# Two stages of a mixture of experts at 376 columns instead of 384, with eight tokens served by fetched rows

## The chip, the cores and the metric

The kernel runs on one core of a Trainium2 chip. The metric is the device time of one execution in microseconds (us), taken as the median of three runs. A core has engines that run side by side, each with its own instruction stream in a fixed order: TensorE (PE, matrix products; PEld is its weight load), VectorE (DVE), ScalarE (ACT), GpSimd (POOL) and SyncE (SP, which here only issues transfers). DMA transfers run on 16 engines of their own.

## The reference, cut to what matters

The reference is two stacked transformer parts on 512 tokens of width 1024. The change lies in the feed-forward part of the first, `peer_ffn`: for every token, 8 heads each choose the best 16 of 16384 single-neuron experts, and the token's output is the sum over its 128 chosen experts.

```python
eidx = jnp.take_along_axis(cidx, fpos, axis=-1).reshape(C, PEER_HEADS * PEER_TOPK)   # 128 experts a token
g = jax.nn.softmax(fv, axis=-1).reshape(C, PEER_HEADS * PEER_TOPK)
u = u_tab[eidx]
a = jax.nn.gelu(jnp.einsum('ted,td->te', u, hb).astype(jnp.float32), approximate=False)
coef = (g * a).astype(hb.dtype)
vv = v_tab[eidx]
return jnp.einsum('te,ted->td', coef, vv)
```

## The kernel before

The kernel has four parts in order: `phase_a` (attention), `phase_peer` (the experts), `phase_conv` and `phase_nsa`. Every large product is done three times on halves of fp32 numbers (`mm3`, lines 178 to 180: high by high, low by high, high by low). Weights arrive as units of 128 x 1024 numbers by SP (`_load`), and each is split (`_split`): ACT writes the high half `whi` (line 102) and DVE the low half `wlo` (line 103).

`phase_peer` serves the first 384 tokens (`ND`) densely and the last 128 by fetching rows:

- **Dense, stage U.** 128 units of the table u; each is multiplied with all 384 tokens (8 blocks of 128 x 3 products of 384 columns), and ACT applies the gelu (line 1215). The results go to DRAM as `Ad`, in 32 groups of 4 units.
- **Gates.** For each token a 128 x 128 table of gate values is made as a product of two one-hot matrices (`gates`, `flush`, line 1105). DVE and ACT build the one-hots (lines 1119, 1123, 1124 and 1126), four tokens at a time. Twelve chunks of 32 tokens come out; ten go to DRAM as `Gd`, the last two stay in `near`.
- **Dense, stage V.** For each of the 128 units of v, `weight` multiplies gates (`gg`, loaded from `Gd`, 640 KB for a group of 4 units, plus two small products for the near chunks, line 1257) with the gelu values, splits the result (`w_hi`, `w_lo`), and 8 x 3 products of 384 columns add into all eight PSUM banks `y`. The v units arrive in a ring of eight 512 KB pieces in memory that stage U's activations held until its last product.
- **Fetched tokens.** `gather` issues 256 indirect transfers on POOL (line 1141): 128 rows of u, then of v, one row for each of the 128 tokens, 512 KB each. A DVE instruction consumes each (lines 1149 and 1159). Three buffers hold u rows, three hold v rows.

What runs beside the products is queued as generators. `pump` and `pump2` take steps from them by credits: `BU` of background work and `GU` (in stage V `GV`) of fetching for each unit; a fetch costs 1.2. A scheduler then orders every engine's instructions by its own simulated timeline, so the order on an engine can differ from the order of the code. `in_turn` adds an order constraint without a wait between engines: before, each fetch's consumer is kept behind the split that was emitted last.

## Time and profile before

| quantity | value |
|---|---|
| median of three runs | 2426.43 us (2426.17 to 2426.85) |
| the profiled execution, its own time | 2425.24 us |
| its span, first to last instruction | 2423.5 us |
| PE busy | 2381.2 us, 98% |
| DVE busy | 1870.4 us, 77% |
| ACT busy | 1149.8 us, 47% |
| mean granted clock of TensorE | 0.991 |

Shares are of the span, so an engine at 77% can be full in one stage and half empty in another. Stage U runs from about 419 to 1037 us and stage V from 1037 to about 1570 us. A busy PE is not a PE at its peak, since its instructions overlap; the spacing of their starts tells the pace. Rows below come from the profile's page and from questions put to the same trace; a line number such as L103 is that of the kernel's file.

### The profile page before, as it was taken

To read this page: it belongs to the slowest core of one execution; us is meant where nothing else is said; L and a number is where in the kernel's file an instruction comes from. 1 tells how busy PE (TensorE), PEld (TensorE's weight loads), DVE (VectorE), ACT (ScalarE), POOL (GpSimd) and SP (SyncE) were. 2 spreads that over 40 slices of the span, in tenths; PEclk is the share of its full clock that TensorE was granted. 3 is DMA by queue.
4 is the path that set the end of the run, shared out by engine and by line. 5 is a ranking of instruction groups with operands and counts; after the bars stand their busy time and mean duration, and the time that the engine had idled before them with its cause. 6 is when DMAs were issued, how large, how long until landed. Compare 5 with 4: busy or idle time off the path is not lost.

```text
span 2423.5 us, 37687 instructions
## 1 busy us (share of the span) xinstructions
PE 2381.2 (98%) x13637; PEld 2163.1 (89%) x13637; DVE 1870.4 (77%) x4198; ACT 1149.8 (47%) x2336; POOL 373.6 (15%) x366
## 2 busy tenths in 40 slices
PE   7999999999999999999999999999999999999998
PEld 5887888999999999999999999988888888887777
DVE  7898579999998978878888887865555436796774
ACT  4467433434777858733333333432222233555772
POOL 0011000014323343324332221100000001000000
PEclk8999999999999999999999999999999999999999
DMA  7460252469989998899999899432223225211002
GB/s 277 145 221 7 75 174 84 161 235 319 335 293 338 349 350 329 276 394 329 382 342 360 319 352 313 165 104 96 96 98 100 98 96 186 91 62 61 1 1 79
DMA packets 170937, 490.47 MB, mean 202 GB/s; under 512 B 15472, under 2 KB 62512, under 8 KB 169088
## 3 DMA queue, kind: packets, MB, share of 16 engines
q1 hardware_dynamic: 123744, 295.48, 35.1%
q0 software_dynamic: 44992, 189.68, 21.5%
q10 hardware_dynamic: 2016, 2.91, 0.4%
q8 instruction: 108, 1.77, 0.3%
q14 instruction: 77, 0.63, 0.1%
HBM read 437.15 MB, written 50.86 MB: 201 GB/s over the span
## 4 chain that ended last, share of the span: by engine, by line
PE 91%; DVE 4%; DMA 2%; ACT 1%; issue 1%; SPq 0%; DVEq 0%; ACTq 0%
PE mm L179 8%; PE mm L180 8%; PE mm L178 8%; PE s L180 8%; PE s L178 8%; PE s L179 8%; PE pt L178 4%; PE pt L180 4%; PE pt L179 4%; PE gp L1105 4%; PE z L178 2%; PE z L180 2%; PE z L179 2%; PE o L1756 2%; PE o L180 2%; PE o L178 2%
## 5 line engine op out<-in xcount | busy, mean ns | idle before, releaser
L102 ACT ACTIVATE whi<-wraw 128x1024 fp32r<-128x1024 f32 (+2 forms) x292 | 305.2, 1046 | 535.0 <-PE mm L179 170.5
L103 DVE TENSOR_TENSOR wlo<-wraw,whi 128x1024 fp32r<-128x1024 f32 (+2 forms) x292 | 351.8, 1206 | 100.4 <-ACT whi L102 98.2
L179 PE MATMUL mm<-act,whi 128*128 128x384 f32 (+2 forms) x1176 | 403.8, 344 | 4.0 <-DVE act L378 4.0
L180 PE MATMUL mm<-act,wlo 128*128 128x384 f32 (+2 forms) x1176 | 402.7, 343 | 0.1
L178 PE MATMUL mm<-act,whi 128*128 128x384 f32 (+2 forms) x1176 | 399.6, 343 | 0.7 <-DVE xres L868 0.7
L102 ACT ACTIVATE whi<-act 128x1024 fp32r<-128x1024 f32 x126 | 133.6, 1061 | 327.9 <-issue 314.0
L179 PEld LDWEIGHTS mm<-act,whi 128*128 128x128 f32 x1176 | 222.7, 189 | 8.1 <-DVE act L378 4.2
L180 PEld LDWEIGHTS mm<-act,wlo 128*128 128x128 f32 x1176 | 222.7, 189 | 4.4 <-DVE wlo L103 0.5
L178 PEld LDWEIGHTS mm<-act,whi 128*128 128x128 f32 x1176 | 220.6, 189 | 4.8 <-issue 0.8
L103 DVE TENSOR_TENSOR wlo<-act,whi 128x1024 fp32r<-128x1024 f32 x126 | 154.2, 1225 | 82.8 <-ACT whi L102 81.5
L1141 POOL DMA_INDIRECT ug<-in_peer_u_rows_dram,eiG x128 | 158.9, 1241 | 363.8 <-DVE ug L1149 246.4
L1141 POOL DMA_INDIRECT vg<-in_peer_v_rows_dram,eiG x128 | 158.3, 1237 | 295.3 <-DVE yG L1159 186.7
L179 PE MATMUL s<-w_lo,whi 128*128 128x384 f32 x512 | 171.1, 334 | 0.3 <-DVE w_lo L224 0.3
L178 PE MATMUL s<-w_hi,whi 128*128 128x384 f32 x512 | 170.4, 334 | 0.8 <-ACT ga L1215 0.6
L180 PE MATMUL s<-w_hi,wlo 128*128 128x384 f32 x512 | 170.5, 334 | 0.0
L1159 DVE SCALAR_TENSOR_TENSOR yG<-vg,gG,yG 128x1024 f32<-128x1024 f32 x127 | 162.7, 1281 | 7.1 <-DMA vg<-in_peer_v_rows_dram,eiG 6.9
L1149 DVE SCALAR_TENSOR_TENSOR ug<-ug,hG 128x1024 f32<-128x1024 f32 x128 | 155.8, 1220 | 6.6 <-DMA ug<-in_peer_u_rows_dram,eiG 6.5
L178 PE MATMUL s<-act,whi 128*128 128x512 f32 x344 | 134.3, 391 | 0.0
L180 PE MATMUL s<-act,wlo 128*128 128x512 f32 x344 | 134.0, 390 | 0.2 <-DVE wlo L103 0.2
L179 PE MATMUL s<-act,whi 128*128 128x512 f32 x344 | 133.6, 389 | 0.0
L1119 DVE TENSOR_SCALAR oh<-iof,idxT 128x128 f32<-128x128 f32 x384 | 117.8, 354 | 9.0 <-PE gp L1105 8.8
L1105 PE MATMUL gp<-oh,oh 128*128 128x128 f32 x768 | 115.0, 274 | 0.0
(700 smaller groups left out, 5722.0 us busy)
## 6 DMA issues: line engine op xcount, KB each, us to landing
wraw<-in_peer_u_dram SPq DMA_DIRECT2D x128, 512.0 KB, 5.0
act<-in_peer_v_rows_dram SPq DMA_DIRECT2D x126, 512.0 KB, 7.2
wraw<-in_a_in_dram SPq DMA_DIRECT2D x64, 512.0 KB, 3.2
Ad<-ga POOLq DMA_DIRECT2D x30, 768.0 KB, 7.4
ga<-Ad SPq DMA_DIRECT2D x30, 768.0 KB, 9.8
Gd<-gc POOLq DMA_DIRECT2D x10, 2048.0 KB, 8.9
gg<-Gd SPq DMA_DIRECT2D x32, 640.0 KB, 7.8
wraw<-in_ada_w_dram SPq DMA_DIRECT2D x32, 512.0 KB, 4.5
```

The lines of the kernel that those rows point to most:

```text
L102: self.first = first = self.nc.scalar.activation(hi[:, :n], r[:, :n], AF.Copy)
L103: self.last = self.nc.vector.tensor_tensor(lo[:, :n], r[:, :n], hi[:, :n].bitcast(F32), op=OP.subtract)
L178: mm(out, lh, rh, start=start, stop=False)
L179: mm(out, lh, rl, start=False, stop=False)
L180: self.product = mm(out, ll, rh, start=False, stop=stop)
L1105: nc.tensor.matmul(gp[:, j, :], o1, o2, start=True, stop=True)
L1119: nc.vector.tensor_scalar(o1, iof, idxT[:, 0, t:t + 1], idxT[:, 2, t:t + 1], op0=OP.is_equal, op1=OP.mult)
L1141: nc.gpsimd.indirect_dma_start(out=t, out_offset=None, in_=tab, in_offset=bass.IndirectOffsetOnAxis(ap=eiG[:, j:j + 1], axis=0))
L1149: c.in_turn(nc.vector.scalar_tensor_tensor(u, u, 1.0, hG, op0=OP.mult, op1=OP.mult, accum_out=aG[:, j:j + 1]))
L1159: op = nc.vector.scalar_tensor_tensor(yG, v, gG[:, j:j + 1], yG, op0=OP.mult, op1=OP.add)
L1756: nc.tensor.matmul(o[64 * h:64 * h + 64, t], V[:, b, v], pair[h][br][:, b * P:(b + 1) * P], start=False, stop=br == 1 and b == qb, skip_gr ...
```

## The change

- `ND` falls from 384 to 376: every product of stages U and V has 376 columns. The eight tokens 376 to 383 are served by rows: each token's 128 experts are spread over 16 groups of partitions (`RX` = 16), so that 8 fetches of u and 8 of v (`gather_x`) do all eight tokens. 32 small transfers on POOL place their indices and gates; `rows_of_x` makes 16 copies of their activations by 8 sums and 8 transposes; at the end 8 small products with `fold` sum the 16 groups into `y`.
- All fetches share four buffers (`NFE`), the credits are 1.75 in stage U and 1.3 in stage V, and the split that is emitted is kept behind the consumer of the fetch that was emitted six (stage V: four) places earlier (`lag`, `paced`, `in_step`).
- The one-hots of four tokens are made by two DVE comparisons of 128 x 512, and ACT scales four of them by the gate.
- The near gates (now two chunks of 28 tokens) are applied in one product instead of two.
- Gates arrive for two groups in one transfer of 1280 KB (two buffers instead of three), and v units in pairs of 1 MB.
- `w_out`'s first four products take their k blocks in the order 0, 1, 2, 4, 5, 6, 7, 3.

```diff
...
-ND = 384
+ND = 376
+N3 = S - P
+XT = N3 - ND
+RX = P // XT
...
-GU, BU, GUL, BUL, GV = 1.6, 2.4, 1.6, 2.4, 1.6
+GU, BU, GUL, BUL, GV = 1.75, 2.4, 1.75, 2.4, 1.3
...
-VB, GB, NGA, W1, FO = 8, 3, 2, 4, 8
+VB, GB, NGA, W1, FO = 8, 2, 2, 4, 8
+NFE = 4
...
         if self.vring is not None and key[0] == "V":
+            if i in self.raw:
+                return
             t = self.vring[self.vnext % len(self.vring)]
             self.vnext += 1
+            if key[1] % 2 == 0:
+                self.raw[i], self.raw[i + 1], view, n = t[:, :1024], t[:, 1024:], t, 2048
+            else:
+                self.raw[i], view = t[:, 1024:], t[:, 1024:]
         else:
-            t = self.wpool.tile([P, 1024], F32, name="wraw", bufs=self.LOAD_AHEAD + 2)
-        view = t[:, :n]
+            t = self.raw[i] = self.wpool.tile([P, 1024], F32, name="wraw", bufs=self.LOAD_AHEAD + 2)
+            view = t[:, :n]
+            if key[0] == "V" and key[1] % 2 == 0:
+                src = src[:, 0, :]
...
         self.last = self.nc.vector.tensor_tensor(lo[:, :n], r[:, :n], hi[:, :n].bitcast(F32), op=OP.subtract)
+        if self.lag is not None and len(self.paced) >= self.lag:
+            self.in_turn(self.last, self.paced[-self.lag])
...
+    def in_step(self, op):
+
+        self.in_turn(op)
+        self.paced.append(op)
...
-    def gemm_w(self, key, out, act, k0=0, start=True, stop=True, pump=3.0):
+    def gemm_w(self, key, out, act, k0=0, start=True, stop=True, pump=3.0, ks=range(KD)):
 
         hi, lo = self.get(key, pump)
-        for k in range(KD):
+        for k in ks:
             c = slice(k * P, (k + 1) * P)
             self.mm3(out, (hi[:, c], lo[:, c]), (act[0][:, k0 + k, :], act[1][:, k0 + k, :]),
-                     start and k == 0, stop and k == KD - 1)
+                     start and k == ks[0], stop and k == ks[-1])
...
-            c.gemm_w(("w_out", m), outs[m], mixed)
+            c.gemm_w(("w_out", m), outs[m], mixed, ks=(0, 1, 2, 4, 5, 6, 7, 3))
...
+            if (tb + 1) * P > ND:
+                eix = pool.tile([P, P], I32, name="eix", bufs=1)
+                nc.vector.tensor_copy(eix, ev)
+                for r in range(RX):
+                    to, sl = slice(r * XT, (r + 1) * XT), slice(r * P // RX, (r + 1) * P // RX)
+                    nc.gpsimd.dma_start(eiX[to, :], eix[P - XT:P, sl])
+                    nc.gpsimd.dma_start(gX[to, :], gv[P - XT:P, sl])
+                c.later2(gather_x())
...
+            tt = slice(tb * P, min(ND, (tb + 1) * P))
+            nc.scalar.activation(idxT[:, :, tt], pt[:, :3 * P].rearrange("p (i t) -> p i t", i=3)[:, :, :tt.stop - tt.start], AF.Copy)
...
-            for ch in range(4):
-                gc = gcpool.tile([P, P, 32], F32, name="gc", bufs=2)
-                near[tb * 4 + ch] = gc
+            for n in range(tb * 4, min(NC_, tb * 4 + 4)):
+                gc = gc2[:, n % 2]
                 prev = None
-                for q in range(8):
-                    hots = []
+                nq = (32 if n < NF_ else NL) // 4
+                for q in range(nq):
+                    t0 = min(n, NF_) * 32 + max(n - NF_, 0) * NL + q * 4
+                    os = [rpool.tile([P, 4, P], F32, name=n, bufs=2) for n in ("oh1", "oh2")]
+                    for i, o in enumerate(os):
+                        nc.vector.tensor_tensor(o, iof[:, None, :].to_broadcast([P, 4, P]),
+                                                idxT[:, i, t0:t0 + 4, None].to_broadcast([P, 4, P]), op=OP.is_equal)
                     for j in range(4):
-                        t = tb * P + ch * 32 + q * 4 + j
-                        o1 = rpool.tile([P, P], F32, name="oh1", bufs=6)
-                        o2 = rpool.tile([P, P], F32, name="oh2", bufs=6)
...
+                        nc.scalar.activation(os[1][:, j, :], os[1][:, j, :], AF.Copy, scale=idxT[:, 2, t0 + j:t0 + j + 1])
+                    hots = [(os[0][:, j, :], os[1][:, j, :]) for j in range(4)]
...
+                flush(prev, gc, nq - 1)
+                if n < NF_:
+                    nc.gpsimd.dma_start(Gd[n], gc.rearrange("p i t -> p (i t)"))
...
+        def rows(tab, idx, j):
+            t = gpool.tile([P, D], F32, name="fetched", bufs=NFE)
+            nc.gpsimd.indirect_dma_start(out=t, out_offset=None, in_=tab,
+                                         in_offset=bass.IndirectOffsetOnAxis(ap=idx[:, j:j + 1], axis=0))
+            return t
...
-                    u = rows(a["peer_u_rows"], j, "ug", 3)
-                    c.in_turn(nc.vector.scalar_tensor_tensor(u, u, 1.0, hG, op0=OP.mult, op1=OP.mult,
+                    u = rows(a["peer_u_rows"], eiG, j)
+                    c.in_step(nc.vector.scalar_tensor_tensor(u, u, 1.0, hG, op0=OP.mult, op1=OP.mult,
...
-                    c.in_turn(op)
+                    c.in_step(op)
...
+        def rows_of_x():
+
...
+                    hs = pool.tile([P, RX, XT], F32, name="stmp", bufs=2)
+                    hh, hl = [act[i][:, kk, None, ND:N3].bitcast(F32).to_broadcast([P, RX, XT]) for i in range(2)]
+                    nc.vector.tensor_tensor(hs, hh, hl, op=OP.add)
...
+                    nc.tensor.transpose(pt[:, k * P:(k + 1) * P], hs.rearrange("p r t -> p (r t)"), c.ident)
...
+        def gather_x():
+
+            n = P // RX
+            for j in range(n):
+                u = rows(a["peer_u_rows"], eiX, j)
+                c.in_step(nc.vector.scalar_tensor_tensor(u, u, 1.0, hX, op0=OP.mult, op1=OP.mult,
+                                                         accum_out=aX[:, j:j + 1]))
+                yield 1.2
...
+        c.later(rows_of_x())
...
+        c.lag = 6
...
-        c.vring = [t.rearrange("p k t -> p (k t)")[:, i * 1024:(i + 1) * 1024] for t in c.act.two(F32) for i in range(4)]
+        c.vring = [t.rearrange("p k t -> p (k t)")[:, i * 2048:(i + 1) * 2048] for t in c.act.two(F32) for i in range(2)]
...
-            gg = vpool.tile([P, NF_, 4, 32], F32, name="gg", bufs=GB)
-            nc.sync.dma_start(gg.rearrange("p c i t -> p c (i t)"),
-                              Gd[0:NF_, :, grp * P:(grp + 1) * P].rearrange("c p n -> p c n"))
+            if grp % 2 == 0:
+                two = vpool.tile([P, NF_, 8, 32], F32, name="gg", bufs=GB)
+                nc.sync.dma_start(two.rearrange("p c i t -> p c (i t)"),
+                                  Gd[0:NF_, :, grp * P:(grp + 2) * P].rearrange("c p n -> p c n"))
+                gates_of[grp], gates_of[grp + 1] = two[:, :, 0:4], two[:, :, 4:8]
...
-            for n in range(NF_, NC_):
-                t = slice(n * 32, n * 32 + 32)
-                nc.vector.tensor_tensor(w[:, t], near[n][:, order[g] * 4 + j, :], ga[:, j, t], op=OP.mult)
+            nc.vector.tensor_tensor(w[:, F_:].rearrange("p (c t) -> p c t", c=2), gc2[:, :, order[g] * 4 + j, 0:NL],
+                                    ga[:, j, F_:].rearrange("p (c t) -> p c t", c=2), op=OP.mult)
...
+        fold = vpool.tile([P, XT], F32, name="fold")
+        nc.vector.tensor_reduce(fold, c.ident.rearrange("p (r t) -> p t r", r=RX), axis=AX.X, op=OP.add)
         weight(0)
+        c.lag = 4
...
-                    nc.tensor.transpose(y[m][:, ND:S], yG[:, m * P:(m + 1) * P], c.ident)
+                    nc.tensor.matmul(y[m][:, ND:N3], yX[:, m * P:(m + 1) * P], fold, start=True, stop=True)
+                    nc.tensor.transpose(y[m][:, N3:S], yG[:, m * P:(m + 1) * P], c.ident)
...
-        c.add_unit(("V", i), v[:, 4 * GRP_V[i // 4] + i % 4, :], 1024)
+        e = 4 * GRP_V[i // 4] + i % 4
+        c.add_unit(("V", i), v[:, e:e + 2, :] if i % 2 == 0 else v[:, e, :], 1024)
...
```

## Rows read from the trace of the kernel before

**Rows 1.** Busy time by stage: PE, PEld, DVE, ACT, POOL, clock, DMA share, GB/s.

```profile
419.00:1037.00 618.00, 617.57 (x3839) 617.11 (x3837) 562.33 (x1377) 402.34 (x954) 187.46 (x176) 1.00 0.83 297
1037.00:1570.00 533.00, 532.32 (x3070) 531.62 (x3071) 443.60 (x830) 190.35 (x262) 152.43 (x120) 1.00 0.91 331
```

**Rows 2.** PE's instructions by shape: count, busy us, mean ns.

```profile
L179 PE MATMUL mm<-act,whi 128*128 128x384 f32 x1024 | 348.2, 340 | 0.0
...
L1105 PE MATMUL gp<-oh,oh 128*128 128x128 f32 x768 | 115.0, 274 | 0.0
```

**Rows 3.** PE in order of time: start us, us; 256, 512 and 384 columns, unbroken runs.

```profile
276.92 0.28 PE L180 MATMUL ps<-act_hi,wlo 128*128 128x256 f32 x1
...
279.40 0.28 PE L180 MATMUL ps<-act_hi,wlo 128*128 128x256 f32 x1
...
404.68 0.39 PE L179 MATMUL mm<-act,whi 128*128 128x512 f32 x1
...
407.40 0.40 PE L179 MATMUL mm<-act,whi 128*128 128x512 f32 x1
...
1020.21 0.34 PE L179 MATMUL mm<-act,whi 128*128 128x384 f32 x1
...
1022.81 0.34 PE L179 MATMUL mm<-act,whi 128*128 128x384 f32 x1
```

**Rows 4.** The chain that ended last: start us, us; eight gate instructions.

```profile
616.15 0.89 PE gp L1105 x8
```

**Rows 5.** Busy time in three parts of stage U, columns as in rows 1.

```profile
419.00:544.00 125.00, 125.00 (x728) 125.00 (x727) 124.93 (x458) 50.69 (x69) 12.68 (x13) 1.00 0.57 196
544.00:740.00 196.00, 196.00 (x1209) 195.90 (x1209) 190.09 (x398) 124.84 (x290) 68.06 (x64) 1.00 0.89 320
740.00:1037.00 297.00, 296.57 (x1906) 296.21 (x1904) 247.31 (x523) 226.82 (x595) 106.72 (x99) 1.00 0.89 326
```

**Rows 6.** DVE's groups in stage U: count, busy us, mean ns, idle before.

```profile
L103 DVE TENSOR_TENSOR wlo<-wraw,whi 128x1024 fp32r<-128x1024 f32 x127 | 155.1, 1221 | 30.1 <-ACT whi L102 29.8
L1119 DVE TENSOR_SCALAR oh<-iof,idxT 128x128 f32<-128x128 f32 x384 | 117.8, 354 | 9.0 <-PE gp L1105 8.8
L1149 DVE SCALAR_TENSOR_TENSOR ug<-ug,hG 128x1024 f32<-128x1024 f32 x67 | 81.5, 1221 | 6.6 <-DMA ug<-in_peer_u_rows_dram,eiG 6.5
L1159 DVE SCALAR_TENSOR_TENSOR yG<-vg,gG,yG 128x1024 f32<-128x1024 f32 x63 | 80.7, 1282 | 7.1 <-DMA vg<-in_peer_v_rows_dram,eiG 6.9
...
L1126 DVE TENSOR_SCALAR oh<-iof,idxT 128x128 f32<-128x128 f32 x96 | 29.1, 304 | 0.0
```

**Rows 7.** DVE's groups by shape, whole trace.

```profile
L592 DVE TENSOR_TENSOR raw<-raw,rsd 128x512 f32<-128x512 f32 x8 | 5.0, 686 | 0.0
```

**Rows 8.** Fetch consumers, lines 1149 and 1159, at the start of stage V (DVE busy).

```profile
1037.00:1200.00 163.00, 30.56 (x51) 1.00 1.00 372
...
1037.00:1200.00 163.00, 19.23 (x15) 1.00 1.00 372
```

**Rows 9.** POOL's group of plain transfers; a u fetch and its us to landing.

```profile
L1217 POOL DMA_DIRECT2D Ad<-ga x30 | 17.1, 569 | 241.3 <-ACT ga L1215 229.9 <-ACT ohd L1123 7.5 <-ACT oh L1124 3.9
...
ug<-in_peer_u_rows_dram,eiG POOLq DMA_INDIRECT x128, 7.2
```

**Rows 10.** Between the stages: two pieces of the chain, then PE.

```profile
1027.59 6.28 DMA gg<-Gd
...
1036.66 8.75 DMA act<-in_peer_v_rows_dram
...
1037.15 0.44 PE L178 MATMUL s<-w_hi,whi 128*128 128x384 f32 x1 [0.58 <-ACT ga L1215]
```

**Rows 11.** PE in order of time, at the first product of `w_out`.

```profile
254.18 0.50 PE L178 MATMUL ps<-act_hi,whi 128*128 128x512 f32 x1 [1.41 <-DVE act_lo L224]
```

**Rows 12.** The consumers of u and v rows: ns min/median/max, first and last start.

```profile
L1149 DVE SCALAR_TENSOR_TENSOR ug<-ug,hG x128: 1172/1220/1290, 544.1 to 1486.2; 128x1024 f32<-128x1024 f32 x128
...
L1159 DVE SCALAR_TENSOR_TENSOR yG<-vg,gG,yG x127: 1269/1280/1298, 598.8 to 1561.1; 128x1024 f32<-128x1024 f32 x127
```

More of the change, by code (lines that the diff above doesn't have):

```diff
@@ L75, in __init__ @@
         self.behind = []
+        self.paced, self.lag = [], None
         self.credit = self.credit2 = 0
@@ L974, in phase_peer @@
         nc.vector.tensor_copy(iob, iof[:, 0:NCAND])
+        hX = gpool.tile([P, D], F32, name="hX")
+        yX = gpool.tile([P, D], F32, name="yX")
+        eiX = gpool.tile([P, P // RX], I32, name="eiX")
+        gX = gpool.tile([P, P // RX], F32, name="gX")
+        aX = gpool.tile([P, P // RX], F32, name="aX")
         hG = gpool.tile([P, D], F32, name="hG")
@@ L1086, in select @@
             i12 = pool.tile([P, 2, P], F32, name="i12", bufs=1)
-            nc.vector.tensor_scalar(i12[:, 1, :], ei[:, 1, :], -1.0, None, op0=OP.mult)
+            nc.vector.tensor_copy(i12[:, 1, :], ei[:, 1, :])
             nc.vector.tensor_copy(i12[:, 0, :], ei[:, 0, :])
@@ L1096, in select @@
             yield from gates(tb)
-        near = {}
+        NF_ = NC_ - 2
+        NL = (ND - NF_ * 32) // 2
+        gc2 = gcpool.tile([P, 2, P, 32], F32, name="gc")
         def gates(tb):
@@ L1154, in gather @@
                 for j in range(16 * h, 16 * h + 16):
-                    v = rows(a["peer_v_rows"], j, "vg", 3)
+                    v = rows(a["peer_v_rows"], eiG, j)
                     if j == 0:
@@ L1179, in rows_of_h @@
                     hs = pool.tile([P, P], F32, name="stmp", bufs=2)
-                    nc.vector.tensor_tensor(hs, act[0][:, kk, ND:S].bitcast(F32), act[1][:, kk, ND:S].bitcast(F32),
+                    nc.vector.tensor_tensor(hs, act[0][:, kk, N3:S].bitcast(F32), act[1][:, kk, N3:S].bitcast(F32),
                                             op=OP.add)
@@ L1184, in rows_of_h @@
                 nc.scalar.activation(hG[:, hf * S:(hf + 1) * S], pt, AF.Copy)
-        sel_left = set(range(ND // P))
+        def rows_of_x():
+            for hf in range(2):
+                pt = psp.tile([P, S], F32, name="tp", bufs=1)
+                for k in range(4):
+                    kk = 4 * hf + k
+                    hs = pool.tile([P, RX, XT], F32, name="stmp", bufs=2)
+                    hh, hl = [act[i][:, kk, None, ND:N3].bitcast(F32).to_broadcast([P, RX, XT]) for i in range(2)]
+                    nc.vector.tensor_tensor(hs, hh, hl, op=OP.add)
+                    yield 0.2
+                    nc.tensor.transpose(pt[:, k * P:(k + 1) * P], hs.rearrange("p r t -> p (r t)"), c.ident)
+                nc.scalar.activation(hX[:, hf * S:(hf + 1) * S], pt, AF.Copy)
+        def gather_x():
[5 more added lines that the diff above has]
+                yield 1.2
+            nc.scalar.activation(aX, aX, AF.Gelu)
+            nc.vector.tensor_tensor(gX, gX, aX, op=OP.mult)
+            for j in range(n):
+                v = rows(a["peer_v_rows"], eiX, j)
+                if j == 0:
+                    op = nc.vector.tensor_scalar(yX, v, gX[:, 0:1], None, op0=OP.mult)
+                else:
+                    op = nc.vector.scalar_tensor_tensor(yX, v, gX[:, j:j + 1], yX, op0=OP.mult, op1=OP.add)
+                c.in_step(op)
+                yield 1.2
+        sel_left = set(range(N3 // P))
         pend = None
@@ L1248, in weight @@
                 for grp in order[g:g + 2]:
-                    if grp not in gates_of:
+                    if grp not in begun:
                         load(grp)
```

30 lines of the change are left out of this document (5 added, 25 removed).

## Prediction

> **What bounds the kernel now.** First the page: PE is busy 98% of the span, but that is an average over four parts, and matmuls overlap, so it doesn't tell what an edit in the experts is worth. Second, busy time by stage [rows 1]: in stage U (618 us) PE lacks 0.4 us, in stage V (533 us) 0.7 us; DVE is at 91% and 83%, ACT at 65% and 36%, DMA at 0.83 and 0.91, the granted clock at 1.00 (2.4 GHz). So no wait is left in either stage that an edit could remove; only less work on PE shortens them. Third, PE in order of time [rows 3], because the spacing of the starts, not the duration, is the price of a product: 15 steps of 384 columns take 2.60 us, 173.3 ns each; 12 steps of 512 take 2.72 us, 226.7 ns each; 21 steps of 256 take 2.48 us, 118 ns each. From 384 to 512 a column costs 53.4 / 128 = 0.417 ns. Check: each stage has 128 units x 8 blocks x 3 = 3072 products (a third of them is a row of its own [rows 2]), and 3072 x 0.1733 = 532.4 us, stage V to the microsecond; stage U has the gates on top.
>
> **What PE saves.** 6144 products lose 8 columns each, 3.33 ns by the slope above: 20.5 us. Gates: eight instructions take 0.89 us [rows 4], 0.111 us each, two for a token (768 for 384 tokens [rows 2]), so eight tokens save 1.8 us. `w_out`: the first product waits 1.41 us for a low half that DVE has just written [rows 11]; if that is block 3's, putting it last saves up to 1.4; if the wait is for the bank, which the same DVE instruction frees, it saves nothing. I take 0.7.
>
> **What PE gains in work.** `rows_of_x`: 8 transposes; bounds 0.11 us (the spacing in [rows 4]) and 0.27 (the duration of such an instruction [rows 2]); I take 0.11, since it lies in a dense stream: 0.9. `fold`: 8 fp32 products of 8 columns, two passes each as for the gates, of 128 columns there; between almost 0 and 0.22 us each; I take 0.22 plus a little for the change of shape: 2.0, in the last 10 us, where nothing covers it.
>
> **What DVE does instead.** One-hots: 384 + 96 instructions take 117.8 + 29.1 = 147 us [rows 6]; now 94 groups of four tokens x 2 comparisons of 128 x 512, at the 686 ns of a two-operand fp32 instruction of that shape [rows 7]: 129 us. A one-operand instruction takes 354 ns for 128 columns, and four of them make 512. The Trainium skill (VectorE: DVE Perf Modes, "The perf-mode tier table") says that an fp32 `tensor_tensor` runs at one element a cycle and a `tensor_scalar` at two, so that the new form is the slower per element. The rows agree: 686 for 512 columns is more than a second 354 would be by that rate, and what is gained comes from the starts, of which four become one. By the rule alone the new comparisons would take longer than the old ones, 188 x 512 columns at half the speed, and DVE would lose what I count as 18 us; the sum on PE would stay as it is. ACT changes from 576 passes to 376 and has a third of the stage free. In stage V one near product replaces two, and products of w lose 8 columns: DVE needs less there. Added: 16 consumers at 1.22 to 1.28 us [rows 6], 20 us over both stages, 8 sums of 128 columns (under half of the 686 ns for 512, about 0.3 each), some copies. In all DVE does no more than before, but the higher rate moves consumers into stage U: 102 units after the first consumer (493 us of 4.83 a unit) x 1.75 / 1.2 = 149, against 130 done there before [rows 6], so 19 x 1.25 = 24 us more, minus 18 for the one-hots: 562 + 24 - 18 = 568 of 618 - 10.2 - 1.8 = 606 us. It fits on average, in 740 to 1037 above all, where DVE idles 50 us [rows 5]. I cost it at nothing for that cover; without it each microsecond of DVE is one of PE.
>
> **The moved waits.** The new order puts each split behind the consumer six (four) fetches back. Behind a late consumer stand, on DVE, the split, and behind that PE; behind the split's buffer, SP's next load. The pace needed: one fetch per 1.2 / 1.75 = 0.69 units of about 4.74 us, 3.3 us; in stage V 1.2 / 1.3 x 4.08 = 3.8 us. The pace that was seen: 66 consumers in 163 us at the start of stage V, 2.5 us each, at a DMA share of 1.00 [rows 8]. Four buffers: 7.2 from issue to landing [rows 9] and 1.25 for the consumer, 8.5 us, and about 10 with the waits in two queues, 2.5 us each. So it holds, with 0.8 us a fetch to spare in U. DMA has room as well: 19 more fetches of 0.52 MB in U are 10 MB on 618 x 297 = 184 MB, a share of 0.88 for 0.83 [rows 1], and V gets as much less. The 32 small transfers stand on POOL's queue between fetches: 32 x 0.57 = 18 us [rows 9], if in one piece. Four buffers and six places of lag cover about 20 us; so the bounds are nothing (a gain is excluded, since no wait of this kind is left) and 18 + 7 - 20 = 5 us; I take 1.5.
>
> **The edge between the stages.** Before, the first gates take 6.28 us to land, and the first v unit of the ring 8.75 us from the end of U; PE waits only 0.58 us and little after [rows 10], so both arrive just in time. Now the first is 1280 KB, not 640, and the second 1 MB, not 512 KB. At stage V's 331 GB/s [rows 1] the extra 640 KB take 2.0 us and the extra 512 KB 1.6; more bytes also stand ahead of the v pair, and a ring piece comes free only when both its units are split. The two units that are already there cover 8.2 us. Bounds: nothing (the edge has the last one-hot one group earlier) to 6.3 + 1.6 (gates that take twice as long, both paid). I take 3.
>
> **The sum** is made on the profiled execution, 2425.24 us, of which 1.7 us lie outside the span. Savings: 20.5 + 1.8 + 0.7 = 23.0. Costs: 0.9 + 2.0 + 1.5 + 3.0 = 7.4. Net 15.6: 2409.6. The median is 1.2 above the profiled execution, so the forecast for it is 2411 us.
>
> **Rival A: products don't shrink.** PEld is busy 617.11 of 618 us and 531.62 of 533 [rows 1]; were the weight load the bound, fewer columns would save nothing, the 20.5 would fall away, and the time would be 2411 + 20.5 = 2431. Against it: at 256 columns the products, each with a load of its own, start every 118 ns [rows 3]. A bound between 170 and 173 ns that 384 columns just touch is hard to place. The Trainium skill (Perfetto Trace Analysis, "Identifying the Most-Contended Engine") tells to judge TensorE by the busy share of LDWEIGHTS; by that rule stages U and V are full of loads, whose number doesn't change, and this rival would hold. The trace disagrees, by the 118 ns. 4 in 100.
>
> **Rival B: DVE becomes the bound early in stage U.** From 419 to 740 it is busy 315 of 321 us [rows 5]. There PE can't run faster than the splits come; the 3.33 ns on each of its 1937 instructions (6 us) would be lost, `rows_of_x` (2.4) and some 5 earlier consumers (6) are added: up to 14 lost, some half if the scheduler defers the selection, as it can. For it: no spare time there. Against: only splits are urgent, and DVE idles later. 2417 to 2425, likeliest 2418; 16 in 100, of which 4 within 0.2%.
>
> **Rival C: the edge costs its upper bound.** 2411 + 5 = 2416; 12 in 100. For it: nothing is early there [rows 10].
>
> **Rival D, slower: the splits wait for fetches through stage U.** Before, 130 consumers took 493 us from the first, at 544.1 us [rows 12], to the stage's end, 3.79 us each, three buffers for a run of u or v rows. Now the order demands 149 - 6 = 143 in 493 - 8.2 - 1.8 = 483 us, 3.38 each. From 3.49 us on, the 15.6 us are gone; from 3.53 on it is slower by 0.2%; at the old 3.79 the stretch takes 542 us and the kernel 2411 - 1.5 + 59 = 2468. For it: DVE idled for landings already (6.6 and 7.1 us [rows 6]) and before, a late consumer held nobody. Against: the old pace was what the credits asked for, and 2.5 us was reached later [rows 8]. 14 in 100. The v rows' last consumer began at 1561.1 us [rows 12], 9 us before the end; a late end of the fetches would cost there too, but fewer are left for V (272 - 149 = 123 at 1.08 a unit, done by unit 114).
>
> **Chances.** Forecast case 52, B 16, C 12, D 14, A 4, other stalls 2, half of them small. The measurement tells about 0.2% (4.9 us) from no change: faster is below 2421.6. Faster: 52 + 12 (of B) + 12 + 1 = 77. Within: 4 (of B) + 2 (of A) + 1 = 7. Slower: 14 + 2 = 16. The range: 2403 (`w_out` in full, `fold` at almost nothing, a free edge, no stalls: 23.7 - 0.9 = 22.8 off 2426.4, rounded down) to 2427, which leaves out D and A. The forecast case alone: 2405 to 2416.
>
> **What would show it.** Products of 376 columns spaced 170 ns (A: 173). Stage V of 128 x 24 x 0.170 = 522 us, stage U about 606 us, PE without gaps inside. 752 gate instructions. In the table of waits, PE behind `wlo` or `whi` should be near zero: a few us at the edge (C), some around 450 to 740 (B), or tens, with DVE idle for `fetched` ahead of `wlo` (D). The forecast is wrong if DVE's idle time before fetch consumers in stage U is above 20 us, or if the stages' sum falls by less than 15 us.

## The result, and the profile after

The change made the kernel slower: 2459.1 us (median of 4 runs, 2457.7 to 2461.3) against 2426.3 before, a ratio of 1.0136 with a 95% interval of 1.0119 to 1.0154. The forecast was 2411. The profiled execution took 2457.66 us, its span is 2455.9.

Busy time of the changed kernel by stage, columns as in [rows 1]; the stages are now 423 to 1060 and 1060 to 1605 us, and a third row is the stretch 590 to 870 us inside stage U:

```profile
423.00:1060.00 637.00, 628.88 (x3857) 624.49 (x3855) 571.59 (x1145) 363.30 (x753) 251.14 (x212) 0.99 0.81 294
1060.00:1605.00 545.00, 533.03 (x3095) 530.52 (x3096) 447.38 (x715) 197.44 (x264) 213.49 (x133) 1.00 0.88 332
590.00:870.00 280.00, 272.53 (x1700) 269.04 (x1699) 250.27 (x394) 180.15 (x410) 130.77 (x119) 0.99 0.84 306
```

Against [rows 1], PE now lacks 8.1 us in stage U and 12.0 in V, where it lacked 0.4 and 0.7. The third row tells most: PE lacks 7.5 us there while DVE is idle for 30 (before, in the same stretch, DVE was busy 261.2 us and PE all 280). So it isn't that DVE has too much work; something at the head of its queue waits, with splits and one-hots behind it.

Second, PE in order of time in stage U, an unbroken run (28 steps between the first and the last row):

```profile
498.73 0.34 PE L197 MATMUL mm<-act,whi 128*128 128x376 f32 x1
498.91 0.33 PE L198 MATMUL mm<-act,whi 128*128 128x376 f32 x1
499.08 0.34 PE L199 MATMUL mm<-act,wlo 128*128 128x376 f32 x1
...
503.58 0.34 PE L198 MATMUL mm<-act,whi 128*128 128x376 f32 x1
```

4.85 us / 28 = 173.2 ns: 376 columns cost what 384 did ([rows 3]: 173.3). The starts alternate between 170 and 177 ns apart. Over stage U the mean of the steps between 150 and 200 ns is 173.2, over stage V 172.1. The forecast had 170.0.

Third, what PE waited for (us in total, times, longest), rows that weren't there before. The first is stage V, the next two are stage U, the last lies ahead of U:

```profile
PE s L199 <- DVE wlo L115: 11.9, 8, 2.2
PE gp L1140 <- ACT oh L1155: 5.3, 7, 1.0
PE mm L199 <- DVE wlo L115: 1.6, 5, 0.5
PE sc L1196 <- ACT s__3431 L1199: 3.8, 1, 3.8
```

So in stage U PE waits mostly for one-hots, and little for splits. These waits are about half of what U lost; the granted clock falls to 0.79 from 700 to 716 us, and behind the waits for one-hots gates start 180 ns apart or more, instead of 111.

Fourth, DVE's groups in stage U, which answer to [rows 6] (count, busy us, mean ns, idle before):

```profile
L1152 DVE TENSOR_TENSOR oh<-iof,idxT 128x512 f32<-128x512 f32 x188 | 118.9, 683 | 29.0 <-PE gp L1140 28.8
L1178 DVE SCALAR_TENSOR_TENSOR fetched<-fetched,hG 128x1024 f32<-128x1024 f32 x73 | 88.2, 1216 | 12.2 <-DMA fetched<-in_peer_u_rows_dram,eiG 11.9
L1188 DVE SCALAR_TENSOR_TENSOR yG<-fetched,gG,yG 128x1024 f32<-128x1024 f32 x63 | 80.5, 1278 | 14.5 <-DMA fetched<-in_peer_v_rows_dram,eiG 14.3
```

DVE waits 28.8 us for PE to release a one-hot buffer and 26.2 us for landings (8.8, and 13.4, before). With the first v row's, which is another instruction, 137 consumers ran in stage U; the rate had asked for 149. Where the consumers of u rows and the eight tokens' last v rows start and end, answering to [rows 12]:

```profile
L1178 DVE SCALAR_TENSOR_TENSOR fetched<-fetched,hG x128: 1173/1217/1283, 552.5 to 1455.7; 128x1024 f32<-128x1024 f32 x128
L1243 DVE SCALAR_TENSOR_TENSOR yX<-fetched,gX,yX x7: 1275/1277/1285, 1560.6 to 1586.0; 128x1024 f32<-128x1024 f32 x7
```

The parts of the span, each from the first product of a stage to the first of the next, in the profiled executions (for stage V to the last product with `w_hi` or `w_lo`):

| | ahead of U | U | V | after V | span |
|---|---|---|---|---|---|
| before | 414.4 | 622.8 | 534.3 | 852.0 | 2423.5 |
| forecast for the change | +0.2 | -10.5 | -7.2 | +2.0 | -15.5 |
| after | 422.8 | 637.4 | 544.7 | 851.0 | 2455.9 |
| measured difference | +8.4 | +14.6 | +10.4 | -1.0 | +32.4 |

### The profile page after: what moved, and what is told of

Same layout as the page of the kernel before. It is cut to its first block, busy times and chain, and to the rows that moved or that the text cites. A ratio compares the mean times of both kernels' runs of the same rounds, so it can differ in the third digit from the quotient of the medians.

```text
span 2455.9 us, 36752 instructions
## 1 busy us (share of the span) xinstructions
PE 2388.7 (97%) x13645; PEld 2163.7 (88%) x13645; DVE 1874.5 (76%) x3813; ACT 1115.0 (45%) x2135; POOL 498.7 (20%) x414
## 4 chain that ended last, share of the span: by engine, by line
PE 85%; issue 6%; DVE 4%; DMA 4%; ACT 1%; SPq 0%; POOL 0%; DVEq 0%; ACTq 0%; POOLq 0%
PE mm L199 8%; PE mm L197 8%; PE mm L198 8%; PE s L199 7%; PE s L197 7%; PE s L198 7%; PE pt L199 3%; PE pt L197 3%; PE pt L198 3%; PE gp L1140 3%; PE o L1824 2%; PE z L199 2%; PE z L197 2%; PE z L198 2%; PE pt L1800 2%
## 5 line engine op out<-in xcount | busy, mean ns | idle before, releaser
L199 PE MATMUL mm<-act,wlo 128*128 128x376 f32 (+2 forms) x1176 | 401.2, 343 | 1.7 <-DVE wlo L115 1.6
L198 PE MATMUL mm<-act,whi 128*128 128x376 f32 (+2 forms) x1176 | 399.1, 340 | 3.5 <-DVE act L397 3.5
L197 PE MATMUL mm<-act,whi 128*128 128x376 f32 (+2 forms) x1176 | 399.1, 343 | 2.0 <-ACT qT L1260 0.7
L1168 POOL DMA_INDIRECT fetched<-in_peer_v_rows_dram,eiG x128 | 205.1, 1602 | 226.4 <-DVE yG L1188 153.7
L1168 POOL DMA_INDIRECT fetched<-in_peer_u_rows_dram,eiG x128 | 195.0, 1523 | 238.3 <-DVE fetched L1178 168.9
L1188 DVE SCALAR_TENSOR_TENSOR yG<-fetched,gG,yG 128x1024 f32<-128x1024 f32 x127 | 162.3, 1278 | 16.0 <-DMA fetched<-in_peer_v_rows_dram,eiG 15.8
L198 PE MATMUL s<-w_lo,whi 128*128 128x376 f32 x512 | 171.3, 335 | 0.0
L197 PE MATMUL s<-w_hi,whi 128*128 128x376 f32 x512 | 170.4, 334 | 0.6 <-ACT ga L1278 0.6
L1178 DVE SCALAR_TENSOR_TENSOR fetched<-fetched,hG 128x1024 f32<-128x1024 f32 x128 | 155.2, 1217 | 14.0 <-DMA fetched<-in_peer_u_rows_dram,eiG 13.6
L199 PE MATMUL s<-w_hi,wlo 128*128 128x376 f32 x512 | 150.4, 336 | 11.9 <-DVE wlo L115 11.9
L115 DVE TENSOR_TENSOR wlo<-act,whi 128x1024 fp32r<-128x1024 f32 x126 | 153.3, 1218 | 5.9 <-ACT whi L114 5.5
L1152 DVE TENSOR_TENSOR oh<-iof,idxT 128x512 f32<-128x512 f32 x188 | 118.9, 683 | 29.0 <-PE gp L1140 28.8
## 6 DMA issues: line engine op xcount, KB each, us to landing
ga<-Ad SPq DMA_DIRECT2D x30, 752.0 KB, 10.4
Gd<-gc POOLq DMA_DIRECT2D x10, 2048.0 KB, 11.5
```

The costliest lines, as they stand in the source:

```text
L115: self.last = self.nc.vector.tensor_tensor(lo[:, :n], r[:, :n], hi[:, :n].bitcast(F32), op=OP.subtract)
L197: mm(out, lh, rh, start=start, stop=False)
L198: mm(out, lh, rl, start=False, stop=False)
L199: self.product = mm(out, ll, rh, start=False, stop=stop)
L1152: nc.vector.tensor_tensor(o, iof[:, None, :].to_broadcast([P, 4, P]), idxT[:, i, t0:t0 + 4, None].to_broadcast([P, 4, P]), op=OP.is_equal)
L1168: nc.gpsimd.indirect_dma_start(out=t, out_offset=None, in_=tab, in_offset=bass.IndirectOffsetOnAxis(ap=idx[:, j:j + 1], axis=0))
```

## The experiments

Theories: (1) the narrower product isn't cheaper; (2) the order that puts each split behind a consumer turns DVE's delays into waits of PE; (3) the eight tokens' 16 fetches, or the fetches' bytes, don't fit. Later: (4) the one-hot buffers, (5) the place of `rows_of_x`. Times are medians, ratios against the kernel before on the same chip; a table of the parts of each span follows at the end. One reservation holds for all: the order on each engine is laid out ahead by a planner, from its own prices, so each variant has an order of its own, and differences of some us between variants can come from that alone.

**Widths by themselves.** A kernel of products alone:

```
for k in range(8): matmul(bank[:, 0:w], whi[:, 128 k : 128 (k+1)], x[:, k, o:o+w])    # 20 times per width, the 8 banks in turn
```

> This kernel computes nothing of the reference: it runs 160 products of each of 23 widths back to back on TensorE, each with its own 128 x 128 weight load, and nothing else. Theory 1, the price rises in steps of the width: 376 columns start every 173.3 ns on average, as 384 do; with a step of 16 columns 368 and 360 take 166.7 and 352 takes 160.0; with a step of 32, 360 and 368 take 173.3 too and 352 takes 160.0. Rival, price by the column (the prediction): 376 takes 170.0, 368 takes 166.7, 360 takes 163.3, 352 takes 160.0. Rival, the weight load is the bound just under 384: all widths from about 350 to 384 take 173.3. Rival, the place in the kernel: here 376 takes 170.0, and a row of 376 columns in a tile of its own or a start at column 8 changes it.

PE in order of time, products of one width grouped (start us, us of the group, and the count): 376 columns and 368 columns of rows of 512 numbers, then 376 columns in a tile with rows of 376:

```profile
389.77 5.01 PE L1895 MATMUL b<-xhi,whi 128*128 128x376 f32 x28
...
334.74 4.83 PE L1895 MATMUL b<-xhi,whi 128*128 128x368 f32 x28
...
657.66 4.75 PE L1895 MATMUL b<-xn,whi 128*128 128x376 f32 x27
```

Less the last product's 0.33 us, 27 steps take 4.68 us (173 ns), 27 take 4.50 (167) and 26 take 4.42 (170). The means over all 159 steps of a width, in ns: 256 columns 120.0, 320 146.7, 336 153.3, 352 161.1, 360 164.5, 364 and 368 166.7, 372 170.0, **376 173.35**, 380 171.1, **384 173.35**, 388 176.7, 400 180.0, 512 227.0. So there is no floor just under 384 (368 columns take 166.7 with a load each), and no clean step of 16 or 32 either: 380 costs less than 376. 376 columns at the price of 384 belong to rows of 512 numbers (173.3 from column 8 too); in rows of 376 they take 170.0, as the forecast had it. But 368 columns get dearer in those same rows of 376 (167.8 instead of 166.7), so a shorter row isn't cheaper as such. 384 columns from column 8 take 176.7. What sets these prices stays open; that the price isn't linear in the width, and depends on how the operand lies in SBUF, is measured.

**No fetches at all.** Both `c.later2(gather...)` are left out, yG and yX set to 0.

> The changed kernel with all 272 row fetches and their consumers left out (the gathered tokens' results are zeros), so nothing but the dense part is left and DMA has about 140 MB less to move. Theory, products of 376 columns cost 173.2 ns in stage U and 171.6 in V whatever the traffic: U 615 to 622 us, V 526 to 530 us, 2412 to 2420 us in all. Rival, the width does save and it is the traffic or the waits that hide it: products every 170.0 ns in both, U 604 to 608, V 522, about 2400 to 2405.

2419.3 us, ratio 0.9970 (0.9960 to 0.9980). Its stages (columns as above):

```profile
416.00:1036.00 620.00, 619.71 (x3858) 618.86 (x3857) 420.29 (x939) 361.72 (x749) 37.19 (x72) 1.00 0.54 186
1036.00:1565.00 529.00, 528.57 (x3090) 528.57 (x3091) 295.81 (x508) 189.25 (x258) 0.00 (x0) 1.00 0.58 208
```

DMA's share falls to 0.54 and 0.58 and PE has no gap left, yet the products start every 173.15 ns in U and 171.57 in V. Theory 1 holds in full for U; V saves about half of the 3.3 ns forecast. V's `w_hi` and `w_lo` already are tiles of 376 columns, so such rows alone don't bring the 170.0 either. It is also a bound: with fetches that cost nothing, the change is worth 0.3%.

**Rows of 376 in stage U**, on the kernel without fetches:

```
-dact = tuple(t[:, :, 0:ND] for t in act)
+dact = two tiles [P, KD, ND], copied from act[:, k, 0:ND] for each k     # rows_of_x and hX left out for the room
```

> The kernel without fetches once more, in stage U the 376 columns of the activations now in tiles of their own, rows of 376 numbers instead of slices of rows of 512 (16 copies on DVE ahead of the stage; the sum over the eight tokens and its transposes are left out too). If the rows' length in SBUF makes the price: products of stage U every 170 to 171.6 ns instead of 173.2, U 610 to 616 us instead of 620.4, 2409 to 2416 us against 2419. If it is the width by itself: 173.2 as before, 2418 to 2424 with the copies.

2416.1 us, ratio 0.9957 (0.9940 to 0.9974). Products of stage U every 172.2 ns instead of 173.15, U 617.2 instead of 620.4: the row's length counts for a part, in the direction of the sweep, but less than expected (170 to 171.6 ns, U 610 to 616), and the 170.0 of the sweep isn't reached inside the kernel.

**368 columns** (`ND = 368`, sixteen tokens by fetches).

> 368 tokens dense instead of 376, sixteen by fetches (32 more fetches than before the change, 16 more than after it). If the price rises in steps of 16 columns: 6144 x 6.67 ns = 41 us less on PE than after the change, 2418 to 2432 with the cost of the fetches. If in steps of 32: no gain, 2459 to 2475. By the column: 20.5 less, 2438 to 2448.

2475.4 us, ratio 1.0199 (1.0181 to 1.0217): at the upper end of the range for no gain, but for another reason. The products did get cheaper, 166.8 ns in U and 167.7 in V; PE waited 32 us for `wlo` and at the end 18.9 for yX.

**All edits but the width** (`ND = 384`, no second gather), with the order of the splits and without it:

> All edits but the width: 384 tokens dense, no eight tokens in a second gather. If the time is lost in the other edits (the order of the splits, the one-hots of four tokens, the larger pieces), about 2448 to 2459 us, PE waiting in both stages as after the change. If the eight tokens' 16 fetches and 32 small transfers lose it, 2424 to 2432. Products of 384 columns every 173.3 ns; if those of 376 cost the same on average, stages U and V are as long as after the change, give or take the waits.

> 384 tokens dense, all other edits, but the splits not placed behind the consumers. Theory: of the 14.7 us that the other edits lose at 384 columns, the order of the splits carries most (PE waited for wlo there, and the one-hots' products for their operands): 2425 to 2432 us, the last consumer after 1540 us, stages U and V near the 619 and 534 us of the kernel before. Rival, the one-hots of four tokens or the larger pieces lose it: stays at 2436 to 2443 with the gaps in front of gp or at the stage's edge.

With the order 2441.1 us, ratio 1.0058 (1.0040 to 1.0076); the forecast of the experiment was 2448 to 2459 or 2424 to 2432, and it lies between. Without it 2432.1, ratio 1.0019 (1.0008 to 1.0030), at the upper edge of its range. So the one-hots of four tokens, the near gates in one product, the larger pieces, the order in `w_out`, the shared buffers and the new rates together cost about 0.2%, and the order of the splits 9 us more. In both kernels 138 consumers start in stage U, so there the 8.3 us between them (630.9 and 622.6) aren't a matter of how many fetches run.

**The change without the order of the splits:**

```
-        c.lag = 6      # stage U
-        c.lag = 4      # stage V
```

> The change without the order that puts each weight split behind a fetch's consumer. If that order makes PE wait for low halves in stage V (8 gaps, 14 us) and some in stage U: 2443 to 2447 us, and the waits of PE for wlo in the s blocks fall from 11.9 us to under 2. Rival, the larger pieces of v and gates bring the splits late: stays at 2457 to 2461 with the same waits.

2482.6 us, ratio 1.0239 (1.0222 to 1.0256): slower still, against both expectations. Stages U (620.9) and V (530.7) run as without fetches, so the waits for `wlo` did come from the order, in V above all, where 150 consumers now cost PE no such wait. In U only 122 consumers start instead of 137, so what U gains is the order and the lower number together. And the fetches now come late, and the end pays. What PE waited for:

```profile
PE s L1350 <- DVE yX L1243: 48.3, 1, 48.3
```

The order isn't a mistake then, but a way to force the fetches to keep up, and it charges PE for it.

**A longer distance** (12 consumers instead of 6 and 4) and **other rates** (`GU = GUL = GV = 1.5`):

> The change with each split 12 consumers back instead of 6 and 4. If the short distance makes the waits (four buffers, a landing time of 8 to 13 us): PE's waits for wlo under 3 us, 2440 to 2448 us, the last consumer within 10 us of 1586. If what limits is how many fetches can be had per microsecond, a longer distance only shifts the delay: 2452 to 2462.

> The change with 1.5 units of credit in all of stages U and V instead of 1.75 in U and 1.3 in V: some 20 fewer consumers demanded in U. If the demand in U is beyond the pace of about 3.8 us a fetch: stage U 620 to 628 us instead of 637, the stages' sum 1160 to 1172, 2437 to 2450 us. If the pace is the same limit in V, what U gains V loses or the end waits for yX: 2455 to 2470.

2471.5 us, ratio 1.0186 (1.0169 to 1.0203), and 2455.5, ratio 1.0123 (1.0110 to 1.0140). The longer distance gave later consumers (last at 1607) and longer waits, worse than both expectations. With 1.5 stage U is 620.1 us, free of waits, and V pays it back with 555.7: the second expectation.

**Five buffers** (`NFE = 5`) and **half the bytes** (rows of 512 numbers, read twice by the consumers):

> The change with five buffers for fetched rows instead of four. Theory, the fetches can't be had faster because DMA has no more to give (its share lies at 0.90 to 0.99 from 800 us on): the last consumer stays within 15 us of 1586, 2450 to 2460 us. Rival, four buffers are too few for a landing time of 8 to 13 us: the pace falls from 3.8 us to near 3.4, PE's waits for wlo vanish, 2435 to 2445.

> The change with each of the 272 fetches taking rows of 512 numbers instead of 1024, from a view of the tables with rows half as long; the consumers read them twice, so that DVE's work stays (the gathered tokens' values are others). It halves the fetches' bytes, 71 of 142 MB less. If the bytes set the fetches' pace: consumers as often as the order asks, PE's waits for wlo under 2 us, stages U and V as without fetches (620 and 529), 2420 to 2428 us. If it is the count of fetches, their descriptors on GpSimd or the order on DVE: 2448 to 2460.

2461.8 us, ratio 1.0147 (1.0130 to 1.0164): a fifth buffer doesn't help, though it takes the waits for landings out of stage U. DVE's groups there:

```profile
L1152 DVE TENSOR_TENSOR oh<-iof,idxT 128x512 f32<-128x512 f32 x188 | 119.5, 683 | 43.2 <-PE gp L1140 43.1
L1178 DVE SCALAR_TENSOR_TENSOR fetched<-fetched,hG 128x1024 f32<-128x1024 f32 x74 | 89.1, 1216 | 1.2 <-issue 1.2
L1188 DVE SCALAR_TENSOR_TENSOR yG<-fetched,gG,yG 128x1024 f32<-128x1024 f32 x63 | 80.4, 1277 | 0.8 <-DMA fetched<-in_peer_v_rows_dram,eiG 0.7
```

DVE waits 0.7 us for landings instead of 26.2, and U still takes 635.0: late landings aren't what U's loss needs. With half the bytes 2447.3, ratio 1.0090 (1.0073 to 1.0107): V is 532.1 us with no wait for `wlo`, the last consumer starts at 1550.9 instead of 1586.0, but U stays at 633.9. Theory 3 explains V at most, not U. And for V the next rows, of the changed kernel, speak for the order in the queue: instructions of ACT, DVE and PE around one of the eight gaps:

```profile
1226.10 0.21 DVE L1319 TENSOR_TENSOR w<-gc,ga 128x56 f32<-128x56 f32 x1
1227.31 1.06 ACT L114 ACTIVATE whi<-act 128x1024 fp32r<-128x1024 f32 x1 [2.23 <-PE s L198]
1229.23 0.55 DVE L243 TENSOR_TENSOR w_lo<-w,w_hi 128x376 fp32r<-128x376 f32 x1 [2.92 <-ACT w_hi L242]
1229.81 0.49 DVE L1317 TENSOR_TENSOR w<-gg,ga 128x320 f32<-128x320 f32 x1
1230.22 0.21 DVE L1319 TENSOR_TENSOR w<-gc,ga 128x56 f32<-128x56 f32 x1
1230.35 1.28 DVE L1188 SCALAR_TENSOR_TENSOR yG<-fetched,gG,yG 128x1024 f32<-128x1024 f32 x1
1231.55 1.22 DVE L115 TENSOR_TENSOR wlo<-act,whi 128x1024 fp32r<-128x1024 f32 x1
1232.82 0.44 PE L199 MATMUL s<-w_hi,wlo 128*128 128x376 f32 x1 [1.47 <-DVE wlo L115]
```

The high half is ready at 1228.37, DVE stands idle until 1229.23, and yet the split runs only at 1231.55, behind the products of w and the consumer, whose 1.2 us are most of PE's 1.47. In stage V DVE waits only 3.1 us in all for fetched rows to land. And all eight gaps come again in the run with the late sums (below), each 1.2 us later from V's start than here (8.5 us here and 9.7 there, 172.7 and 173.9, on to 516.6 and 517.8), though its stage U is 24 us longer: the order laid ahead sets them, not the time at which a row lands. Whether the half rows helped by landing sooner or by the other order that the planner then laid isn't separated.

**Without the eight tokens' fetches**, all else as changed:

> The change with the last token block's 256 fetches and the order of the splits, but without the eight tokens' 16 fetches, their consumers and their 32 small transfers (these tokens' results are zeros). If those 16 fetches are what the stages can't hide: 2430 to 2440 us, some 5 us under the same edits at 384 columns (2441). If the order alone loses nearly all: 2450 to 2458.

2466.3 us, ratio 1.0162 (1.0145 to 1.0179), slower than with them (part of it one wait of 7.2 us for a high half, at 1022 us), and outside both expectations. Its consumers of v rows (first and last start):

```profile
L1188 DVE SCALAR_TENSOR_TENSOR yG<-fetched,gG,yG x127: 1259/1277/1317, 619.7 to 1535.1; 128x1024 f32<-128x1024 f32 x127
```

The last one starts 81 us before stage V ends, and PE waits all the same (11.5 us for `wlo` in V): in V it isn't the number of fetches that costs, it is the place of the consumers ahead of the splits. Theory 3 falls for the 16 fetches as long as the order stands; when the order is gone, the end waits 48.3 us for their sums (above), and not at all at 384 columns without them.

**Three one-hot buffers, late sums for the eight tokens, and both with lower rates** (`bufs=3`; `c.later(rows_of_x())` moved behind the score products; `GU = GUL = 1.5, GV = 1.35`):

> The change with three buffers for each of the two one-hot tiles of four tokens instead of two. Stage U is 15 us longer than without the order of the splits, and fewer bytes did not help there. If DVE's waits for a one-hot buffer (28.8 us), with the splits behind them, are the cause: those waits fall under 10 us, PE's gaps between 670 and 870 us go, stage U 622 to 627 us, 2444 to 2450 us. If the cause is the number of consumers that the order asks for: U 632 to 640, 2454 to 2462.

> The change with the sums and transposes for the eight tokens' rows put behind the score products instead of ahead of them. If their transposes in the middle of the score products make the 3.8 us wait and the low clock after it ahead of stage U: no wait of a score product for its bank, granted clock 1.00 from 360 to 425 us, the first product of stage U at 415 to 418 us instead of 422.8, 2450 to 2453 us. If not: 2457 to 2461 with the same wait.

> The change with the late sums of the run before, three one-hot buffers, 1.5 units of credit in stage U and 1.35 in V. If the three losses add up (8 us ahead of U, 15 in U) and V stays at 545: 2434 to 2440 us. If V pays for the consumers that U leaves over, as it did with 1.5 in both (556): 2444 to 2452. In no case under 2426, since the kernel without any fetch takes 2419.

2464.5 us, ratio 1.0162 (1.0145 to 1.0179); 2473.0, ratio 1.0200 (1.0183 to 1.0217); 2471.5, ratio 1.0195 (1.0178 to 1.0212). None helps, and all lie above what was expected of them. With three buffers DVE's wait for one-hots falls from 28.8 to 11.3 us and U from 637.4 to 631.7; V takes it back. With the late sums the stage ahead of U is repaired (411.7 instead of 422.8) and U grows to 661.3. The eight transposes now stand at 484 to 499 us, where PE has no gap; DVE is busy for only 65 of the 100 us from 450 to 550 (99.9 in the changed kernel), and PE's gaps come from 595 us on. What shifts the work so isn't shown. With both, U is 635.8 although the rate is 1.5, and the end waits 13.9 us for yX.

The stretch that the late sums repair, in the changed kernel, PE in order of time and the busy time of 361 to 376 us:

```profile
361.62 0.38 PE L1225 MATMUL tp<-ident,stmp 128*128 128x128 f32 x2
365.79 2.08 PE L1196 MATMUL sc<-skT,qT 128*128 128x128 f32 x8 [3.79 <-ACT s__3431 L1199]
...
369.58 0.63 PE L199 MATMUL mm<-act,wlo 128*128 128x512 f32 x1
370.00 0.63 PE L197 MATMUL mm<-act,whi 128*128 128x512 f32 x1
...
361.00:376.00 15.00, 10.52 (x43) 8.48 (x42) 14.07 (x91) 3.69 (x6) 0.00 (x0) 0.77 0.10 36
```

After the last transposes of `rows_of_x`, PE waits 3.79 us for the bank of the score products. Then the granted clock falls from 2.4 to 1.2 GHz for a while (0.77 on average over these 15 us), and products of 512 columns start 427 ns apart instead of 227. With the sums moved, the clock is 1.00 there and PE has no gap. In the kernel without fetches the sums stand at the same place of the code, and yet PE has no gap and the clock is 1.00 (361 to 376 us); so neither the work of the sums nor their place in the code makes the wait by itself; the order that the planner laid around them has a part in it.

The parts of the spans, in us (before and after as above). They are those of one execution of each kernel, which can lie some us off its median (three one-hot buffers: 2456.8 for a median of 2464.5):

| kernel | ahead of U | U | V | after V |
|---|---|---|---|---|
| no fetches | 416.1 | 620.4 | 529.0 | 851.7 |
| no fetches, rows of 376 in U | 418.7 | 617.2 | 529.0 | 850.8 |
| 368 columns | 427.3 | 631.4 | 538.9 | 877.3 |
| 384 columns, other edits | 416.1 | 630.9 | 542.9 | 851.7 |
| the same without the order | 415.6 | 622.6 | 536.2 | 851.9 |
| change without the order | 423.6 | 620.9 | 530.7 | 905.9 |
| distance 12 | 422.7 | 632.8 | 551.6 | 859.8 |
| rates 1.5 | 423.9 | 620.1 | 555.7 | 850.9 |
| five buffers | 424.0 | 635.0 | 549.8 | 850.3 |
| half the bytes | 425.1 | 633.9 | 532.1 | 851.2 |
| without the 16 fetches | 424.8 | 642.0 | 549.7 | 851.1 |
| three one-hot buffers | 422.4 | 631.7 | 549.9 | 851.0 |
| late sums | 411.7 | 661.3 | 545.8 | 851.1 |
| late sums, buffers, rates | 415.5 | 635.8 | 546.6 | 871.4 |

## Why the prediction was wrong, step by step

- **What bounds the kernel.** Right: PE gap-free in both stages, only less work on PE shortens them. The new gaps (8.1 us in U, 12.0 in V) are part of the loss.
- **What PE saves, the products: the first step that failed.** The slope of 0.417 ns a column was read between 384 and 512, widths at which it does hold (173.35 and 227.0 in the sweep), and carried to 376. There the price was 173.2 in U and 172.1 in V: of 20.5 us, U saved nothing to speak of and V 3072 x (173.36 - 172.1) = 4. 16.5 us of the forecast were never there. Rival A had this outcome, for a reason that didn't hold: 368 columns start every 166.7 ns, each with its load, so the weight load is no floor. The Trainium skill (Perfetto Trace Analysis, "Identifying the Most-Contended Engine") asks to judge TensorE by the busy share of its weight loads, beside its share of the peak rate. Read as a bound set by the loads, as rival A read it, the sweep disagrees: PEld is busy all the time at 368 columns and at 376, and the pace is 166.7 and 173.35.
- **Gates and `w_out`.** 752 gate instructions, as forecast. `w_out` still waits 1.41 us for a low half at its first product ([rows 11]): the reorder is worth 0, not 0.7. `fold` and the transposes cost nothing visible: after V the span is 1.0 us shorter, not 2.0 longer.
- **`rows_of_x`: mis-sized.** 0.9 us was the price of eight transposes, costed as if they lay in a dense stream. Of the 8.4 us lost ahead of U about 7 are theirs (at 384 columns, without them, 416.1): a wait for a bank and the low clock after it, both gone with the late sums.
- **What DVE does instead.** The sum was right (one-hots 118.9 us busy for 129 forecast, DVE 571.6 us in U for 568), and it didn't matter: PE waits in U while DVE idles for 65 us. Where DVE has no spare time, from 423 to 550 us, PE lacks nothing, so rival B didn't come. The prediction says that its rows show the new comparisons to be the slower form per element; they don't, since none has the old form at 512 columns. DVE waits 28.8 us for a one-hot buffer (two buffers of four tokens for six of one) and 26.2 for landings, the latter above the 20 that the prediction had named as refuting it. But neither wait by itself is the loss. Without the order, and with the order at 1.5 units, DVE waits as long for one-hots, and U takes 620.9 and 620.1 us:

```profile
L1152 DVE TENSOR_TENSOR oh<-iof,idxT 128x512 f32<-128x512 f32 x188 | 121.0, 686 | 32.5 <-PE gp L1140 30.6 <-ACT idxT L1126 1.4
L1152 DVE TENSOR_TENSOR oh<-iof,idxT 128x512 f32<-128x512 f32 x188 | 121.2, 688 | 30.5 <-PE gp L1140 28.9 <-ACT idxT L1126 1.2
```

  And with five buffers the landings' wait is gone and U is 635.0. A total of idle time doesn't tell which of it PE pays for.
- **The moved waits: the second step that failed.** Costed at 1.5 us with bounds 0 to 5, because the pace that was seen, 2.5 us a fetch at the start of stage V, left 0.8 us a fetch to spare. That pace was a misreading: the 51 and 15 of [rows 8] are instructions, and line 1149 has two for each u row, the product and the reading of its sum. The same 163 us of the kernel before, by operation:

```profile
L1149 DVE SCALAR_TENSOR_TENSOR ug<-ug,hG 128x1024 f32<-128x1024 f32 x26 | 31.6, 1220 | 0.0
L1159 DVE SCALAR_TENSOR_TENSOR yG<-vg,gG,yG 128x1024 f32<-128x1024 f32 x15 | 19.2, 1282 | 0.0
L1149 DVE DVE_READ_ACCUMULATOR ug<-ug,hG 128x1 f32 x25 | 2.1, 84 | 0.0
```

  41 consumers in 163 us are 4.0 us each, slower than the 3.3 and 3.8 that the prediction took the order to ask for in U and V: read rightly, the trace before the change showed no room at all, and the argument against rival D falls with it. In stage U of the changed kernel 137 consumers took 508 us, 3.71 each; the quickest stage U of any run with whole rows, at 384 columns without the order, came to 3.57 (138 in 492). Against the run without the order U is 16.5 us longer (637.4 and 620.9) and V 14.0, and that run pays 48.3 at the end. This is rival D, in part: it gave 2468 us for splits that wait behind late fetches, and got 14 in 100. That the order of the splits costs this is shown by the runs without it, in U at the higher rate alone: with 1.5 units the order is still there and U takes 620.1. That the fetched rows must be late for it isn't shown (the five buffers in U, the 3.1 us of landings in V speak against it). Its second place (V) was thought to be covered, and wasn't.
- **The edge.** As forecast in size: the first product of V waits 0.57 us (0.58 in [rows 10]) and two gaps by 1075 us add 2.7, the first behind a piece of v that ACT waited 1.93 us for:

```profile
1060.11 0.44 PE L197 MATMUL s<-w_hi,whi 128*128 128x376 f32 x1 [0.57 <-ACT ga L1278]
...
1066.95 2.01 ACT L114 ACTIVATE whi<-act 128x1024 fp32r<-128x1024 f32 x2 [1.93 <-DMA act<-in_peer_v_rows_dram]
...
1068.59 0.44 PE L199 MATMUL s<-w_hi,wlo 128*128 128x376 f32 x1 [1.38 <-DVE wlo L115]
```

In sum, against the forecast: 16.5 us of savings that weren't there, 8.2 ahead of U, 15.0 in U (16.5 less the 1.5 allowed), 11.0 in V (14.0 less the edge's 3.0), less 3.0 after V: 47.7 of the 48 us between 2411 and 2459. That it adds up so closely is chance, since the run without the order also has fewer consumers in U and an order of its own. The prediction had named as its refutation that the stages' sum falls by less than 15 us; it rose by 25.

Open: which rule makes 376 columns of longer rows cost what 384 do; and through which of DVE's waits the order reaches PE in U. With three one-hot buffers the wait for one-hots falls to 11.3 us and U by 6, with five buffers for rows the landings go and U falls by 2, and in both trials the other wait grows and the order changes with it.

## What to carry to other kernels

Take a price from the very width, row length and place that you will use: a slope between two widths told nothing of a third that lay 8 columns beside one of them. When an order ties work that PE needs to work that waits for memory, cost it by the pace that is held over the whole stage, count the work itself and not the instructions on its line (66 of them were 41 fetches), and look at what stands ahead of the urgent work in its queue, not at the engine's total. And before spending on a narrower dense part, run it with the other part free of charge: here that bound was 0.3%.

## What the runs showed of the hardware

- Products of 376 columns start at intervals that alternate (170 and 177 ns), and their mean depends on how the moving operand lies: 173.35 ns in rows of 512, 170.0 in rows of 376, with nothing else running. For 368 columns it is the other way round: 166.7 and 167.8.
- A start 8 columns into the row leaves 376 columns at 173.3 and takes 384 from 173.35 to 176.7; 380 columns cost less (171.1) than 376.
- Around the 3.79 us wait of PE ahead of U (0.69 and 0.56 us more follow it) the granted clock averages 0.77 over 15 us, and 512-column products start 427 ns apart after it, at 1.2 GHz. By estimate that is 6.9 us at the lower level and 3.4 us lost, beside the 5.0 of waits. The stretch of 700 to 716 us averages 0.79, with three waits of PE of 0.4 to 1.0 us in it. The single waits of up to 2.3 us in stage V leave the clock at 1.00.
- A DVE instruction that also sums its products leaves two records on its line, the second of about 80 ns: a count of records on that line is twice the count of the work.
